# Modulation sums queued one chunk later, the gate summed in its own tile, and 24 modulation steps per sub-layer

## The chip, the cores and the metric

The kernel runs on one core of one Trainium2 chip. The metric is the device time of one launch in microseconds (us); the time before is the median of three runs.

## The reference, cut to what matters

Two layers of three sub-layers each: a half-step SwiGLU feed-forward, a token mixer (layer 0: sparse attention beside a gated delta rule, called "hybrid"; layer 1: multi-head latent attention), and another feed-forward. Every sub-layer is wrapped by a conditioning on one vector `c`:

```
cs  = silu(c)                                        # (1024,)
mod = cs @ mod_w[layer] + mod_b[layer]               # 9 x 1024: per sub-layer shift, scale, gate
x   = layer_norm(alpha * x + (1 + gate) * f(x * (1 + scale) + shift), ln_g, ln_b)
```

`x` is 256 x 1024, `mod_w[layer]` 1024 x 9216, a feed-forward has 2816 hidden columns; all is float32. The change concerns only how `cs @ mod_w + mod_b` (the modulation) is computed and when.

## The kernel before, in words

The six sub-layers si = 0 ... 5 run one after the other: feed-forward, hybrid, feed-forward, feed-forward, latent attention, feed-forward. A feed-forward (`ffn`) goes through 11 chunks of two tiles of 128 hidden columns. A chunk's gate and up products (matmuls into four banks of tag "gu", L263 to L265) are followed by silu on ScalarE (L548, `sg`), the product on VectorE (L551), a split of `h` in two parts, and, behind the next chunk's gate and up products, the down products (`acc<-hd,h`). Weights are split in two parts on ScalarE (L258) and VectorE or GpSimd (L259).

The modulation is a generator, `mod_gen`, that the sub-layers drive. For each sub-layer and each of scale (i = 1), shift (0) and gate (2), in this order, it makes eight steps: load 128 rows of `mod_w` (a 128 x 1024 tile, 512 KB, tag "wd" with three buffers, shared with the tiles of `ffn_w_down`), multiply by a column of `cs` and add into an accumulator (VectorE, L218 for the first step, L225 for the others). The accumulator (tag "macc", one buffer) then holds 128 partial rows; `mod_sums` adds them over the partitions at once. For scale and shift that is `mod_cols`: eight transposes on TensorE (L138) into two "gu" banks, and two reductions on VectorE (L139). For the gate it is `mod_gate`: two products with a matrix of ones (L180) into two "gu" banks, and on VectorE (L182) the sum is added to a tile G, which a DMA (L212) has filled with the gate's bias; G has two buffers. The epilogue of the sub-layer reads G (L381).

`pace` decides how many steps are traced beside which piece of a sub-layer. Its aim for the end of each sub-layer is a running count of steps, `goals`; inside a sub-layer the share grows with the tiles (feed-forward), with 14 "beats" (hybrid) or with the 16 heads (latent attention, eight of them for the whole share). When the share passes 1, `need` runs the generator until this sub-layer's gate and the next one's scale and shift are done.

The order on each engine is not the order of the program's text. A planner takes the instructions by the order in which they were traced, and issues an instruction on its engine as soon as, by the planner's own times, its inputs and a buffer are there; what was traced later fills the pauses of what was traced earlier, and may run far ahead of its place. Buffers of one tag are given out in the order of tracing. `behind(m)` lets what is traced in it be issued only behind the instruction `m` of the same engine. On the chip every engine then works through its queue in order: an instruction that waits holds up all behind it. `last_mm` is the last matmul that `mm3` has traced.

## Time and profile before

| what | value |
|---|---|
| median of three runs | 1216.07 us (1212.24 to 1216.48) |
| span of the profiled execution | 1212.3 us |
| VectorE busy | 905.5 us, 75% of the span |
| GpSimd busy | 255.4 us, 21% |
| moved by DMA | 259.76 MB, mean 214 GB/s |

The span runs from the first to the last instruction of one profiled execution. The page shows no time outside it; the median of the runs is 3.8 us above the span, and the fastest run lies 0.06 us below it. So the profiled execution's own time is taken as its span, and a difference worked out from its rows is applied to the median. In the rows, PE is TensorE, PEld its weight loads, DVE is VectorE, ACT is ScalarE, POOL is GpSimd, SP the queue that issues the DMAs. A line such as L225 is a line of the kernel.

### The profile page before, as it was taken

How to read it: one execution, taken by the hardware profiler on the slowest of the kernel's cores; microseconds unless marked ns; L12 is line 12 of the kernel's file. 1: busy time of each engine (PE TensorE's matmuls, PEld its weight loads, DVE VectorE, ACT ScalarE, POOL GpSimd, SP SyncE). 2: the span in 40 equal slices, each digit the busy share in tenths (PEclk: the TensorE clock that was granted, in tenths of full speed). 3: DMA queues.
4: the chain of work that ended last, by engine and by line, in shares of the span. 5: the costliest groups of instructions: out<-in, count | busy, mean ns of one | idle time of the engine just before them, and what ended most of it. 6: DMA issues, size and time to landing. Idle time of an engine off the chain costs nothing.

```text
span 1212.3 us, 19687 instructions
## 1 busy us (share of the span) xinstructions
PE 1135.4 (94%) x7783; PEld 1035.5 (85%) x7783; DVE 905.5 (75%) x1376; ACT 547.6 (45%) x959; POOL 255.4 (21%) x186
## 2 busy tenths in 40 slices
PE   4998999999899998999999899899989998999997
PEld 3897999788787887989999889799978878899995
DVE  6699777698985677878885888778788438866545
ACT  0644444456433445533543543334456556544430
POOL 0631000224731452320000322000221234300001
PEclk9999999999999999999999999999999998999999
DMA  9779999454310586788997488889725135876620
GB/s 352 249 260 345 303 319 303 145 165 123 98 36 5 188 274 212 243 291 297 325 307 238 139 283 284 269 297 302 266 79 168 66 105 180 295 250 189 215 72 35
DMA packets 155334, 259.76 MB, mean 214 GB/s; under 512 B 8813, under 2 KB 117354, under 8 KB 155242
## 3 DMA queue, kind: packets, MB, share of 16 engines
q1 hardware_dynamic: 155050, 258.45, 63.9%
q8 instruction: 61, 1.00, 0.3%
q14 instruction: 31, 0.25, 0.1%
q10 hardware_dynamic: 192, 0.05, 0.0%
HBM read 257.43 MB, written 1.05 MB: 213 GB/s over the span
## 4 chain that ended last, share of the span: by engine, by line
PE 51%; DVE 22%; DMA 13%; ACT 5%; issue 5%; POOL 3%; SPq 0%; POOLq 0%; DVEq 0%; ACTq 0%
PE gu L265 8%; PE gu L264 8%; PE gu L263 7%; DMA wd<-ffn_w_down 7%; PE acc L265 6%; PE acc L263 6%; PE acc L264 6%; DVE macc L225 3%; DMA wd<-mod_w 3%; DMA w<-ffn_w_up 2%; DVE g L259 2%; POOL hd L259 2%; PE gu L732 2%; DVE u L259 2%; ACT hd L258 1%
## 5 line engine op out<-in xcount | busy, mean ns | idle before, releaser
L225 DVE SCALAR_TENSOR_TENSOR macc<-wd,csT,macc 128x1024 f32<-128x1024 f32 x112 | 169.0, 1509 | 27.1 <-DMA wd<-mod_w 26.5
L263 PE MATMUL gu<-uT,g 128*128 128x256 f32 x640 | 181.1, 283 | 1.4 <-ACT sg L548 1.4
L265 PE MATMUL gu<-uT,g 128*128 128x256 f32 x640 | 181.2, 283 | 1.2 <-DVE g L259 1.2
L265 PE MATMUL gu<-uT,u 128*128 128x256 f32 x640 | 181.2, 283 | 1.0 <-DVE u L259 1.0
L263 PE MATMUL gu<-uT,u 128*128 128x256 f32 x640 | 181.1, 283 | 0.0
L264 PE MATMUL gu<-uT,u 128*128 128x256 f32 x640 | 181.1, 283 | 0.0
L264 PE MATMUL gu<-uT,g 128*128 128x256 f32 x640 | 181.1, 283 | 0.0
L258 ACT CAST hd<-wd 128x1024 fp32r<-128x1024 f32 x88 | 92.2, 1049 | 136.8 <-DMA wd<-ffn_w_down 118.9
L263 PE MATMUL acc<-hd,h 128*128 128x512 f32 x352 | 141.3, 401 | 1.5 <-ACT h L258 1.5
L265 PE MATMUL acc<-hd,h 128*128 128x512 f32 x352 | 137.6, 391 | 1.1 <-DVE h L259 1.1
L264 PE MATMUL acc<-hd,h 128*128 128x512 f32 x352 | 137.7, 391 | 0.0
L259 DVE TENSOR_TENSOR g<-w,g 128x1024 fp32r<-128x1024 f32 x86 | 118.9, 1386 | 22.8 <-ACT g L258 22.3
L263 PEld LDWEIGHTS gu<-uT,g 128*128 128x128 f32 x640 | 122.7, 192 | 3.2 <-ACT sg L548 1.8
L265 PEld LDWEIGHTS gu<-uT,g 128*128 128x128 f32 x640 | 122.7, 192 | 1.6 <-DVE g L259 1.6
L264 PEld LDWEIGHTS gu<-uT,g 128*128 128x128 f32 x640 | 122.7, 192 | 1.4
L265 PEld LDWEIGHTS gu<-uT,u 128*128 128x128 f32 x640 | 122.9, 192 | 1.2 <-DVE u L259 1.2
L263 PEld LDWEIGHTS gu<-uT,u 128*128 128x128 f32 x640 | 122.9, 192 | 0.0
L264 PEld LDWEIGHTS gu<-uT,u 128*128 128x128 f32 x640 | 122.9, 192 | 0.0
L259 DVE TENSOR_TENSOR u<-w,u 128x1024 fp32r<-128x1024 f32 x81 | 104.1, 1290 | 24.5 <-ACT u L258 24.3
L258 ACT CAST u<-w 128x1024 fp32r<-128x1024 f32 (+1 forms) x89 | 91.6, 1039 | 62.7 <-DMA w<-ffn_w_up 51.9
L259 POOL TENSOR_TENSOR hd<-wd,hd 128x1024 fp32r<-128x1024 f32 x32 | 86.6, 2712 | 141.6 <-ACT hd L258 141.6
L259 POOL TENSOR_TENSOR hl<-w,hl 128x1024 fp32r<-128x1024 f32 x28 | 72.5, 2602 | 202.2 <-ACT hl L258 201.7
(392 smaller groups left out, 2495.2 us busy)
## 6 DMA issues: line engine op xcount, KB each, us to landing
wd<-mod_w SPq DMA_DIRECT2D x130, 512.0 KB, 4.8
wd<-ffn_w_down SPq DMA_DIRECT2D x88, 512.0 KB, 4.6
w<-ffn_w_gate SPq DMA_DIRECT2D x43, 1024.0 KB, 8.3
w<-ffn_w_up SPq DMA_DIRECT2D x43, 1024.0 KB, 6.9
w<-hyb_w_in SPq DMA_DIRECT2D x16, 1024.0 KB, 6.1
w<-mod_w SPq DMA_DIRECT2D x7, 1024.0 KB, 7.5
w<-hyb_w_out SPq DMA_DIRECT2D x4, 1024.0 KB, 4.9
w<-mla_w_out SPq DMA_DIRECT2D x4, 1024.0 KB, 5.4
```

The costliest lines, as they stand in the source:

```text
L225: step = nc.vector.scalar_tensor_tensor(acc, w, c, acc, ALU.mult, ALU.add)
L258: i = self.nc.scalar.copy(hi, src)
L259: return i, (eng or self.nc.vector).tensor_tensor(out=lo, in0=src, in1=hi.bitcast(F32), op=ALU.subtract)
L263: nc.tensor.matmul(out, lh, rh, start=first, stop=False)
L264: nc.tensor.matmul(out, lh, rl, start=False, stop=False)
L265: self.last_mm = nc.tensor.matmul(out, ll, rh, start=False, stop=last)
L732: nc.tensor.matmul(pt[:, b * S : (b + 1) * S], q[:, b * P : (b + 1) * P], k, start=True, stop=True)
```

## The change: what it does

- `mod_sums` no longer follows its last step directly. When the eighth step is traced, the generator notes the last matmul traced so far (`held`) and stops; `pace` does not go on until `mm3` has traced another one. Then the sums are traced `behind` the newest matmul, on whichever engine they share with it (TensorE). `need` does not look at `held`.
- The gate is summed in its own tile: the accumulator is a tile of tag "G" (now one buffer), filled with the bias by DMA and multiplied by 1/128 on ScalarE, so that the sum over partitions holds the bias once. All eight steps are multiply-adds (L225). `mod_gate` copies the bank to that tile with 1 added, on ScalarE; the VectorE additions are gone.
- Scale and shift use "macc" with two buffers, for the first sub-layer too.
- `goals` 44, 64, 98, 132, 136, 144 become 40, 64, 88, 112, 136, 144: after the first, 24 steps in each sub-layer but the last, which has 8. In latent attention the share is spread over 14 heads rather than 8.
- Comments are removed, in many places; these hunks are left out here.

```diff
     def pace(self, part):
-        """runs the modulation up to its share of what this sub-layer takes of it"""
+
         goal = self.base + math.ceil((self.goal - self.base) * min(part, 1.0))
-        while self.count < goal:
+        while self.count < goal and (self.held is None or self.held is not self.last_mm):
+            self.held = None
             self.count += next(self.bg)
...
-    def mod_gate(self, si, acc, G):
-        """G holds the bias"""
+    def mod_gate(self, si, acc):
+
         nc = self.nc
         for h in range(2):
             pt = self.bank("gu")
             nc.tensor.matmul(pt, self.one, acc[:, h * 512 : (h + 1) * 512], start=True, stop=True)
-            g = G[:, h * 512 : (h + 1) * 512]
-            nc.vector.scalar_tensor_tensor(g, pt, 1.0, g, ALU.add, ALU.add)
-        self.G[si] = G
+            nc.scalar.activation(acc[:, h * 512 : (h + 1) * 512], pt, AF.Copy, bias=1.0)
+        self.G[si] = acc
...
-                acc = self.tl(self.wp, [P, D], "G", bufs=2) if si == 0 and i < 2 else self.tl(self.wp, [P, D], "macc")
                 if i == 2:
-                    G = self.tl(self.wp, [P, D], "G", bufs=2)
-                    nc.sync.dma_start(G, t["mod_b"][l, off : off + D].partition_broadcast(P))
+
+                    acc = self.tl(self.wp, [P, D], "G")
+                    nc.sync.dma_start(acc, t["mod_b"][l, off : off + D].partition_broadcast(P))
+                    nc.scalar.mul(acc, acc, 1.0 / P)
+                else:
+                    acc = self.tl(self.wp, [P, D], "macc", bufs=2)
...
-            if k == 0:
+            if k == 0 and i < 2:
                 nc.vector.tensor_scalar_mul(acc, w, c)
...
-            self.mod_sums(si, i, acc, G, step)
+            if self.last_mm is not None:
+                self.held = self.last_mm
+                yield 0
+                with self.behind(self.last_mm):
+                    self.mod_sums(si, i, acc, step)
+            else:
+                self.mod_sums(si, i, acc, step)
             self.mdone.add((si, i))
...
-            vs = self.tl(self.wp, [P, 2, 2, W], "macc")
+            vs = self.tl(self.wp, [P, 2, 2, W], "macc", bufs=2)
...
-        self.marks, self.last_mm = [None], None
+        self.marks, self.last_mm, self.held = [None], None, None
         self.left = None
-        goals = (44, 64, 98, 132, 136, 144)
+        goals = (40, 64, 88, 112, 136, 144)
...
-                T.pace((4 * g + i + 1) / 8)
+                T.pace((4 * g + i + 1) / 14)
```

## Rows read from the trace of the kernel before

**Rows 1.** The page, part 1: engine, busy us, share of the span, instructions.
```profile
PE 1135.4 (94%) x7783; PEld 1035.5 (85%) x7783; DVE 905.5 (75%) x1376; ACT 547.6 (45%) x959; POOL 255.4 (21%) x186
```
**Rows 2.** Busy time by stretch: stretch, length, engines, granted clock, DMA share, GB/s.
```profile
36.00:234.00 198.00, 191.59 (x1330) 177.87 (x1330) 157.71 (x208) 89.26 (x122) 37.12 (x50) 0.99 0.82 275
...
234.00:300.00 66.00, 59.16 (x398) 54.64 (x397) 57.78 (x138) 39.71 (x85) 19.88 (x10) 0.92 0.52 157
300.00:394.00 94.00, 86.55 (x643) 73.73 (x642) 72.67 (x152) 36.62 (x96) 40.13 (x28) 0.98 0.16 48
394.00:468.00 74.00, 72.77 (x464) 60.64 (x463) 52.65 (x78) 38.09 (x78) 34.13 (x15) 1.00 0.68 234
...
478.00:670.00 192.00, 188.83 (x1325) 176.53 (x1326) 150.03 (x177) 86.65 (x128) 25.15 (x12) 0.99 0.80 272
...
680.00:882.00 202.00, 194.59 (x1357) 181.54 (x1358) 162.11 (x190) 87.13 (x131) 29.42 (x14) 0.99 0.80 269
...
1010.00:1196.00 186.00, 184.68 (x1304) 173.85 (x1304) 115.34 (x139) 83.89 (x123) 22.71 (x10) 0.99 0.55 181
```
**Rows 3.** TensorE's timeline at four sums: start, us, line, tiles, [idle before <-releaser].
```profile
94.51 0.28 PE L265 MATMUL gu<-uT,u 128*128 128x256 f32 x1
98.99 3.65 PE L180 MATMUL gu<-macc,one 128*128 128x512 f32 x4 [4.19 <-DVE macc L225]
...
523.54 1.95 PE L180 MATMUL gu<-macc,one 128*128 128x512 f32 x4 [0.86 <-DVE macc L225]
...
559.90 0.63 PE L138 MATMUL gu<-ident,macc 128*128 128x128 f32 x4 [0.44 <-DVE macc L225]
561.27 0.66 PE L138 MATMUL gu<-ident,macc 128*128 128x128 f32 x4 [0.75 <-DVE sg L551]
...
761.49 0.66 PE L138 MATMUL gu<-ident,macc 128*128 128x128 f32 x4 [0.90 <-ACT sg L548]
765.16 1.11 PE L138 MATMUL gu<-ident,macc 128*128 128x128 f32 x4 [3.01 <-DVE sg L551]
```
**Rows 4.** Busy time by stretch, the two stretches of half clock (columns as Rows 2).
```profile
98.99:102.42 3.43, 3.43 (x5) 1.46 (x5) 2.20 (x5) 2.68 (x4) 0.00 (x0) 0.50 1.09 367
764.60:768.00 3.40, 2.84 (x9) 2.46 (x10) 3.40 (x7) 1.75 (x4) 0.00 (x0) 0.50 0.95 283
```
**Rows 5.** ScalarE's timeline before the sum at 761 us.
```profile
760.11 1.05 ACT L258 CAST u<-w 128x1024 fp32r<-128x1024 f32 x1 [7.21 <-DMA w<-ffn_w_up]
761.06 0.38 ACT L548 ACTIVATE sg<-gu 128x256 f32<-128x256 f32 x1
```
**Rows 6.** Tile macc: count, ns min/median/max, first and last start us, shapes.
```profile
L225 DVE SCALAR_TENSOR_TENSOR macc<-wd,csT,macc x112: 1271/1281/3431, 62.0 to 1133.4; 128x1024 f32<-128x1024 f32 x112
...
L218 DVE TENSOR_SCALAR macc<-wd,csT x16: 736/746/2241, 61.2 to 1019.0; 128x1024 f32<-128x1024 f32 x16
```
**Rows 7.** Tile G: its VectorE addition, and its DMA's landing.
```profile
L182 DVE SCALAR_TENSOR_TENSOR G<-gu,G x12: 675/684/692, 102.6 to 1189.9; 128x512 f32<-128x512 f32 x12
...
DMA to landing us min/median/max: 3.7/4.7/8.9
```
**Rows 8.** ScalarE groups: count, busy us, mean ns, idle before and its releasers.
```profile
L258 ACT CAST h<-sg 128x256 fp32r<-128x256 f32 x82 | 32.9, 405 | 146.3 <-DVE sg L551 146.3
...
L745 ACT COPY PT<-gu 128x512 f32<-128x512 f32 x12 | 7.0, 586 | 9.3 <-PE gu L743 9.3
...
L790 ACT ACTIVATE x<-x 128x1024 f32<-128x1024 f32 x2 | 2.0, 1052 | 0.0
```
**Rows 9.** VectorE's timeline: last step before, and first step after, the gated delta rule.
```profile
216.74 1.28 DVE L225 SCALAR_TENSOR_TENSOR macc<-wd,csT,macc 128x1024 f32<-128x1024 f32 x1
...
405.63 1.99 DVE L218 TENSOR_SCALAR macc<-wd,csT 128x1024 f32<-128x1024 f32 x1
```
**Rows 10.** TensorE's timeline: the gate sum of the hybrid.
```profile
403.11 1.88 PE L180 MATMUL gu<-macc,one 128*128 128x512 f32 x4
```
**Rows 11.** VectorE's timeline: the epilogue's last reading of G before the hybrid.
```profile
236.27 0.75 DVE L381 SCALAR_TENSOR_TENSOR tmp<-acc,G 128x256 f32<-128x256 f32 x2
```
**Rows 12.** GpSimd's timeline in the gated delta rule.
```profile
293.21 12.64 POOL L259 TENSOR_TENSOR hl<-w,hl 128x1024 fp32r<-128x1024 f32 x5 [10.24 <-ACT hl L258]
```
**Rows 13.** Busy time by stretch of latent attention (columns as Rows 2).
```profile
920.00:990.00 70.00, 68.79 (x479) 61.38 (x477) 34.80 (x107) 40.47 (x101) 14.34 (x6) 1.00 0.32 107
904.00:920.00 16.00, 14.00 (x105) 12.95 (x104) 15.63 (x40) 10.17 (x22) 6.07 (x11) 1.00 0.36 108
```

More of the change, by code (lines that the diff above doesn't have):

```diff
@@ L189, in mod_gen @@
         todo = [(si, i, k) for si in range(len(self.subs)) for i in (1, 0, 2) for k in range(KD)]
-        ws, loaded, G, step = {}, 0, None, None
+        ws, loaded, step = {}, 0, None
         def load(si, i, k):
@@ L234, in mod_gen, with mod_sums @@
                 self.load_x()
-    def mod_sums(self, si, i, acc, G, step):
+    def mod_sums(self, si, i, acc, step):
         if i == 2:
-            self.mod_gate(si, acc, G)
+            self.mod_gate(si, acc)
         elif i == 1:
```

## The prediction

> **What bounds the kernel now.** I read first the page's engine shares, then the busy times by stage, then TensorE's timeline wherever a modulation sum stands in it. TensorE is busy 1135.4 of 1212.3 us; ScalarE has 45% [rows 1]. So a change on VectorE or ScalarE pays only where TensorE stood still for it. The stages show where that can be. In the last feed-forward (8 modulation steps) TensorE is busy 184.68 of 186 us, 1.3 us idle. The first has 6.4 us idle (198 less 191.59), the third sub-layer 3.2 (192 less 188.83), the fourth 7.4 (202 less 194.59) [rows 2]. These three carry most of the steps, so I looked there at each sum.
>
> Four sums made TensorE wait, in two ways [rows 3]. The reader is to look at the bracket behind a row.
> - For the last step itself (releaser `macc`): 4.19 us at 98.99, 0.86 at 523.54, 0.44 at 559.90, together 5.49.
> - For a "gu" bank (releaser `sg`): the two banks of a sum are those that the chunk's own silu and product must first empty. 0.75 us at 561.27, 0.90 and 3.01 at 761.49 and 765.16, together 4.66.
>
> The two longest were followed by stretches with the granted clock at 0.50, that is 1.2 instead of 2.4 GHz, of 3.43 and 3.40 us [rows 4]; each costs about half its length, 1.7 us. So the sums' places hold 5.49 + 4.66 + 3.4 = 13.6 us. This is the most that the change can gain in the feed-forwards.
>
> **The change part by part.**
>
> *Sums a chunk later.* In a feed-forward `last_mm` changes once a chunk, so a held sum stands behind the next chunk's gate and up products. A chunk lasts about 17 us (an estimate: the 186 us of the last feed-forward over 11 chunks [rows 2]). The step that was late by 4.19 us will have ended long before. All the `macc` waits go: 5.49 us, and the first half-clock stretch with them, 1.7. What is late next at that place is the bank: the sum still stands directly behind a chunk's products and still needs the first two banks, so the `sg` waits are not touched by the placing. They hang on how far ScalarE and VectorE lag. At 761 ScalarE had stood 7.21 us for a tile of `ffn_w_up`, with the silu queued behind it [rows 5]: a late DMA, in a stage whose DMA share is 0.80 against 0.55 in the last feed-forward [rows 2]. Ten of its modulation tiles go (5.2 MB of the 54 MB or so that 269 GB/s over 202 us make), so this gets rarer, not impossible. Bounds: none of 4.66 + 1.7 = 6.4 us, or all. I take half, 3.2. Gain of the placing: 5.5 + 1.7 + 3.2 = 10.4 us.
>
> *The gate in its own tile.* Per gate VectorE loses two additions of 0.684 us [rows 7] and its first step grows from 0.746 to 1.281 [rows 6]: 0.83 us less, 5 us over six gates. TensorE does not wait for these in a feed-forward, so nothing is booked. ScalarE gains per gate a multiplication of 128 x 1024, 1.05 us by the nearest row, and two copies out of a bank at 0.59 [rows 8]: 2.2 us, 13 over six. It stood 146.3 us for `sg` alone [rows 8]; that idle time hides it. Without that cover a gate would cost its 2.2 us.
>
> The multiplication is a new wait on ScalarE, for the bias DMA, which lands 4.7 us after issue in the median and 8.9 at most [rows 7]. Queued behind it stand casts and silu, and TensorE waits for these. The DMA is traced ahead of the gate's weight tiles and is normally early. Bounds 0 and 8.9 us once; I take 0. On SP the same DMA now waits for the only G buffer, until the epilogue before has read it; behind it on SP stand the following weights. The epilogue of the first feed-forward reads G last at 236.27 [rows 11], and the hybrid's modulation is traced after that, so the wait is short.
>
> *24 steps per sub-layer.* The feed-forwards lose 4, 10 and 10 steps, the hybrid gains 4 and latent attention 20. Where VectorE is not what TensorE waits for, the steps saved are worth nothing.
>
> In the hybrid the place changes more than the number. Before, VectorE ran no step between 216.74 and 405.63 [rows 9], because the single `macc` buffer was held until the gate sum got its banks at 403.11 [rows 10]; after it 16 steps ran beside attention. Now the gate's eight steps can start only behind 236.27 (one G), and scale and shift have two more buffers. The planner fills VectorE's pauses with whatever has its inputs; the four gate steps traced in the hybrid already ran before 217 us. So part of the 24 steps can move into the gated delta rule (234 to 394), where VectorE is busy 57.78 of 66 and 72.67 of 94 us and TensorE idles 6.8 and 7.5 us [rows 2]. No row shows a step there. The nearest row is attention, 394 to 468: with 16 steps among its work TensorE idled 74 less 72.77 = 1.23 us in all, at most 0.08 per step. By this 24 steps cost 1.9 us. From above, a step that delays TensorE by its full 1.281 us costs that much each; with 16 of them in the delta rule, 20.5 us. From below, everything that TensorE idled in attention, 1.2 us, could be won. I take 1.9, the nearest row.
>
> In latent attention VectorE is full early (15.63 of 16 us, 904 to 920) and half idle later (34.80 of 70, 920 to 990) [rows 13]. 24 steps are 31 us, 1.7 steps per head, and 35 us are free from 920 on. The planner has them behind the heads, so few fall into the full stretch. By the same 0.08 the cost is 1.9 us. Bounds: 0, and for six steps that all delay TensorE in the full stretch, 7.7. The sums there (gate, scale, shift) are TensorE work that moved from the feed-forward before, so it cancels.
>
> *Sum*: 10.4 gained, 1.9 + 1.9 lost: 6.6 us less. On the profiled span 1212.3 gives 1205.7; on the median, 1216.07 less 6.6 = 1209.5.
>
> **A rule that speaks against it.** A step's median is 1.281 us, its longest 3.431 [rows 6], and GpSimd works 12.64 us without a pause from 293.21 in the delta rule [rows 12]. By the Trainium skill (SBUF — State Buffer, "Who interferes with whom") a VectorE instruction with two SBUF inputs and a GpSimd instruction that reads SBUF share a port, and the later one waits for the whole of the other. The long steps agree with it; it would put 3.4 instead of 1.3 us on a step that lands in such a stretch. Whether steps land there no run has shown; this is part of the second rival.
>
> **The rivals.**
>
> *The bank waits stay, and the result drowns.* For it: both kinds of wait end at the same place, and the `sg` waits depend on silu, which the change does not hurry; after a hold `pace` catches up three or four steps in a row (4 x 1.281 = 5.1 us on VectorE), which can make `sg` late elsewhere. Against it: less DMA in these stages. Then the gain is 5.5 + 1.7 = 7.2, less 3.8: 3.4 us, 1212.7.
>
> *Steps in the gated delta rule (slower).* Mechanism: the freed buffers let steps run from 240 to 394, and the short chain between VectorE and TensorE there is lengthened at each. Price: 1.281 us a step. 16 steps cost 20.5; with 1.9 in latent attention and 10.4 gained that is 12 us more, 1228. It turns the sign from (10.4 - 1.9) / 1.281, about 7 such steps, on. For it: TensorE's 14 us of idle time show that it waits there, and VectorE has few pauses. Against it: these steps go only where the planner sees a pause, and a delay can be swallowed by projections that TensorE has queued between.
>
> *All waits at sums go and attention pays nothing*: 13.6 us less, 1202.5. For it: attention's TensorE hardly idles. Against it: some bank wait always remains.
>
> **How the numbers follow.** The runs of the kernel spread over 0.35%; about 0.5% (6.1 us) can be told from no change. Chances: forecast 0.35 (1209.5, its own range 1204 to 1213), all waits gone 0.13, bank waits stay 0.30, delta rule slower 0.22. The forecast stands just beyond 0.5%, so a part of it (0.06) counts as no change, and a part of the slower rival (0.03) with few steps too. Faster 0.42, within 0.5% 0.39, slower 0.19. The range goes from 1200 (the 13.6 us and a little DMA relief) to 1225 (close to the slower rival), leaving out about 0.1 on either side.
>
> **What the profile after would show.** Right: no bracket "DVE macc" before L138 or L180 on TensorE in a feed-forward; no half clock at the first gate sum; idle time of TensorE in the fourth sub-layer well under 7 us; steps within latent attention with TensorE's idle time there up by no more than 2 us. Wrong, first rival: brackets with `sg` before the sums, as long as now. Wrong, second rival: L225 rows between 240 and 394 us, and the stretches 234 to 300 and 300 to 394 longer by over 5 us. The forecast falls altogether if a new wait of several us on ScalarE for the bias DMA shows up.

## The result: 2.6% slower, where 0.5% faster was forecast

The changed kernel takes 1247.37 us in the median of four runs (1243.07 to 1254.21), the kernel before on the same chip 1216.28 (1212.24 to 1219.44): a ratio of 1.026, interval 1.023 to 1.0291. That is 31 us more where 6.6 less were forecast, and 22 us beyond the range's end.

The profiled execution has a span of 1252.4 us against 1212.3. It is the slowest of the changed kernel's four runs (mean granted clock 0.965, where the fastest, 1243.07 us, has 0.976), so the stages below add up to 40 us of difference where the medians show 31. I cut both into stages at TensorE's first transposes of each sub-layer's input rows (`gu<-ident,x`), and added up TensorE's idle time and the stretches of granted clock 0.50 (1.2 GHz) in each. Lengths in us, before to after; the other columns are worked out in the same way:

| stage | length | difference | TensorE idle | at clock 0.50 |
|---|---|---|---|---|
| first feed-forward | 214.8 to 217.5 | +2.7 | 8.2 to 9.3 | 3.4 to 6.8 |
| hybrid | 239.6 to 260.8 | **+21.2** | 16.2 to 27.2 | 13.7 to 37.5 |
| second feed-forward | 201.2 to 203.3 | +2.2 | 4.0 to 6.8 | 3.4 to 6.8 |
| third feed-forward | 207.2 to 206.0 | -1.2 | 10.5 to 8.8 | 3.4 to 6.8 |
| latent attention | 123.1 to 136.4 | **+13.3** | 9.9 to 13.4 | 0.5 to 17.1 |
| last feed-forward | 204.8 to 206.8 | +2.0 | 10.4 to 12.0 | 10.3 to 11.9 |

I count half of a stretch at half clock as lost, an estimate from the two granted clocks, 0.50 and 1.00. In the hybrid 11.0 us more of idle time and half of 23.8 us more of half clock give 22.9, near the 21.2; in latent attention 3.5 and half of 16.6 give 11.8 of 13.3. So of this execution's 40 us the two attentions lost about 34, and by this count some 20 of them by the clock.

The page's part 1 of after, to compare with [rows 1]: VectorE works no more than before, TensorE 22 us more in as many matmuls.

```profile
PE 1157.3 (92%) x7783; PEld 1054.1 (84%) x7783; DVE 905.9 (72%) x1364; ACT 562.4 (45%) x977; POOL 262.6 (21%) x186
```

The busy times by stretch (stretch, length, PE, PEld, DVE, ACT, POOL, granted clock, DMA share, GB/s). The hybrid is cut at the last matmul of the scan (the loop over four chunks of rows that ends the gated delta rule). First the kernel before:

```profile
236.40:392.60 156.20, 143.72 (x1025) 126.97 (x1026) 128.05 (x285) 74.41 (x175) 60.01 (x37) 0.96 0.31 94
392.60:476.00 83.40, 79.76 (x503) 66.55 (x502) 60.16 (x90) 39.75 (x83) 37.25 (x17) 1.00 0.68 231
```

And after, with the latent attention and a feed-forward behind it that answer to [rows 2, 13]:

```profile
239.00:409.10 170.10, 148.39 (x1039) 131.27 (x1040) 147.27 (x299) 76.25 (x177) 60.68 (x37) 0.94 0.44 135
409.10:499.80 90.70, 85.20 (x489) 70.86 (x489) 47.75 (x81) 40.93 (x84) 35.97 (x17) 0.91 0.51 174
...
704.00:906.00 202.00, 195.19 (x1351) 181.79 (x1350) 149.65 (x172) 92.61 (x140) 30.83 (x14) 0.98 0.70 234
...
922.00:1026.00 104.00, 95.65 (x635) 86.41 (x634) 87.41 (x189) 52.91 (x130) 29.09 (x22) 0.95 0.64 212
```

The reader is to see two things. The delta rule has 19 us more of VectorE work (147.27 against 128.05: 14 modulation steps) and lasts 14 us longer. But the rest of the hybrid has 12 us *less* VectorE work and still lasts 7 us longer, with the granted clock at 0.91 instead of 1.00. "So many more steps" can't be the whole cause.

**What the forecast had looked at** did happen. TensorE's timeline at the first gate sum, and what ended TensorE's idle time before all the transposes of the sums [rows 3]:

```profile
131.23 2.28 PE L181 MATMUL gu<-G,one 128*128 128x512 f32 x4
```

```profile
L139 PE MATMUL gu<-ident,macc x80: 270/273/329, 190.4 to 1020.8; 128*128 128x128 f32 x80
its engine sat idle before it (us, times) until:
  DVE sg L560: 0.2, 1
```

No `macc` bracket is left, the `sg` waits are 0.2 us instead of 4.66, and the clock at the first gate sum stays at 1.00. Other waits of the same size stand elsewhere in the feed-forwards: transposes for the rotary angles waiting for a bank, and a silu behind a late tile of `ffn_w_up`. Half clock of 3.4 us follows the first (from 138.02), and 6.8 us begins within the second (from 530.56).

```profile
137.66 0.33 PE L680 MATMUL gu<-ident,cs 128*128 128x128 f32 x1 [4.03 <-DVE sg L560]
...
532.54 0.58 PE L272 MATMUL gu<-uT,g 128*128 128x256 f32 x1 [4.47 <-ACT sg L557]
```

**In the delta rule** VectorE's timeline shows the steps that [rows 9] had none of: six of the gate from 247.35 to 301.68 and eight of scale from 308.31 to 385.34. ScalarE's multiplication of the bias stands at the very head of the hybrid, among the casts of its input.

```profile
247.35 1.28 DVE L228 SCALAR_TENSOR_TENSOR G<-wd,csT,G 128x1024 f32<-128x1024 f32 x1 [0.68 <-ACT G L213]
...
301.68 3.00 DVE L228 SCALAR_TENSOR_TENSOR G<-wd,csT,G 128x1024 f32<-128x1024 f32 x1
308.31 2.61 DVE L221 TENSOR_SCALAR macc<-wd,csT 128x1024 f32<-128x1024 f32 x1 [0.29 <-DMA wd<-mod_w]
...
385.34 1.28 DVE L228 SCALAR_TENSOR_TENSOR macc<-wd,csT,macc 128x1024 f32<-128x1024 f32 x1
```

```profile
246.26 1.06 ACT L213 ACTIVATE G<-G 128x1024 f32<-128x1024 f32 x1
```

**At the end of the delta rule** the last normalisation (`decT`, four instructions on VectorE) takes 7.50 us, beside three GpSimd splits (of weights, L268) of 7.15 us together; attention's first logits (`lg`) are behind it on VectorE, and TensorE waits 3.14 us for them. The granted clock is then 0.50 for 17 us, in which TensorE is never idle. VectorE, GpSimd, TensorE and the stretch:

```profile
415.01 7.50 DVE L1315 SCALAR_TENSOR_TENSOR decT<-decT,oss,ngz 128x128 f32<-128x128 f32 x4 [8.58 <-POOL oss L120]
422.55 0.42 DVE L745 CUSTOM_DVE_ANT_0 lg<-gu,sc 128x256 f32<-128x256 f32 x1
```

```profile
414.95 7.15 POOL L268 TENSOR_TENSOR hl<-w,hl 128x1024 fp32r<-128x1024 f32 x3
```

```profile
423.67 0.44 PE L752 MATMUL gu<-ident,lg 128*128 128x128 f32 x2 [3.14 <-ACT lg L750]
```

```profile
424.70:441.80 17.10, 17.10 (x64) 13.51 (x63) 4.37 (x11) 4.29 (x11) 0.00 (x0) 0.50 0.28 104
```

Before, the same normalisation ran from 396.29 for 5.47 us while TensorE still had projections queued until the gate sum at 403.11 [rows 10], and no `lg` was due:

```profile
396.29 5.47 DVE L1306 SCALAR_TENSOR_TENSOR decT<-decT,oss,ngz 128x128 f32<-128x128 f32 x4 [6.56 <-POOL oss L119]
```

**In latent attention** two steps stand on VectorE beside the division of four heads (L762, L764), and the transposes behind it wait 1.89 us; 3.4 us at 0.50 begin at 967.46, as this wait ends, and 3.4 more follow a wait of 1.61 us at 990. VectorE and TensorE:

```profile
964.78 1.28 DVE L228 SCALAR_TENSOR_TENSOR G<-wd,csT,G 128x1024 f32<-128x1024 f32 x1
965.98 0.20 DVE L762 RECIPROCAL sums<-sums 128x8 f32<-128x8 f32 x1
966.10 0.70 DVE L221 TENSOR_SCALAR macc<-wd,csT 128x1024 f32<-128x1024 f32 x1
966.83 0.69 DVE L764 TENSOR_TENSOR PT<-acc,sums 128x512 f32<-128x512 f32 x1
```

```profile
967.58 1.11 PE L768 MATMUL gu<-ident,PT 128*128 128x128 f32 x4 [1.89 <-DVE PT L764]
```

Before, no step ran in latent attention, and of these transposes the longest wait there was 0.31 us. The other half clock in this stage does not stand behind the division: 6.8 us at its head (from 909.44), ahead of its first step at 918.5, and 3.4 us at 933.33.

### The profile page after: what moved, and what is told of

It reads as the page before. It is cut to its first block, busy times and chain, and to the rows that moved or that the text cites. A ratio compares the mean times of both kernels' runs of the same rounds, so it can differ in the third digit from the quotient of the medians.

```text
span 1252.4 us, 19669 instructions
## 1 busy us (share of the span) xinstructions
PE 1157.3 (92%) x7783; PEld 1054.1 (84%) x7783; DVE 905.9 (72%) x1364; ACT 562.4 (45%) x977; POOL 262.6 (21%) x186
## 4 chain that ended last, share of the span: by engine, by line
PE 60%; DVE 20%; DMA 9%; ACT 4%; issue 4%; POOL 3%; SPq 0%; POOLq 0%; DVEq 0%; ACTq 0%
PE gu L272 10%; PE gu L274 10%; PE gu L273 10%; PE acc L274 7%; PE acc L272 7%; PE acc L273 7%; DVE G L228 2%; PE gu L741 2%; DMA wd<-ffn_w_down 2%; DMA wd<-mod_w 2%; DMA w<-ffn_w_gate 2%; DVE g L268 2%; DVE u L268 1%; DMA w<-ffn_w_up 1%; DMA w<-mod_w 1%
## 5 line engine op out<-in xcount | busy, mean ns | idle before, releaser
L274 PE MATMUL acc<-hd,h 128*128 128x512 f32 x352 | 140.0, 398 | 3.1 <-DVE h L268 3.1
L272 PE MATMUL acc<-hd,h 128*128 128x512 f32 x352 | 141.7, 402 | 0.0
L273 PE MATMUL acc<-hd,h 128*128 128x512 f32 x352 | 140.0, 398 | 0.0
L268 DVE TENSOR_TENSOR g<-w,g 128x1024 fp32r<-128x1024 f32 x86 | 118.5, 1383 | 25.8 <-ACT g L267 25.8
L228 DVE SCALAR_TENSOR_TENSOR macc<-wd,csT,macc 128x1024 f32<-128x1024 f32 x72 | 97.1, 1349 | 43.7 <-DMA wd<-mod_w 43.3
L268 DVE TENSOR_TENSOR u<-w,u 128x1024 fp32r<-128x1024 f32 x81 | 104.0, 1288 | 28.1 <-ACT u L267 28.0
L268 POOL TENSOR_TENSOR hl<-w,hl 128x1024 fp32r<-128x1024 f32 x28 | 72.6, 2600 | 230.1 <-ACT hl L267 230.1
L268 POOL TENSOR_TENSOR hd<-wd,hd 128x1024 fp32r<-128x1024 f32 x32 | 88.2, 2764 | 121.2 <-ACT hd L267 121.2
```

Source lines behind the costliest of these rows:

```text
L228: step = nc.vector.scalar_tensor_tensor(acc, w, c, acc, ALU.mult, ALU.add)
L268: return i, (eng or self.nc.vector).tensor_tensor(out=lo, in0=src, in1=hi.bitcast(F32), op=ALU.subtract)
L272: nc.tensor.matmul(out, lh, rh, start=first, stop=False)
L273: nc.tensor.matmul(out, lh, rl, start=False, stop=False)
L274: self.last_mm = nc.tensor.matmul(out, ll, rh, start=False, stop=last)
```

## The experiments

Ratios are against runs of the kernel before on the same chip, whose medians were 1214.13 to 1217.03 us. The profiled execution gives each stage's length; differences from before in us (FF: feed-forward). Each stage difference comes from one execution, while the ratios come from four to six runs of a kernel (two for sums at once, short steps and no loads). Where the two disagree, the ratio is the firmer number:

| kernel | ratio [95%] | FF 1 | hybrid | FF 2 | FF 3 | latent | FF 4 |
|---|---|---|---|---|---|---|---|
| changed kernel | 1.0260 [1.0230, 1.0291] | +2.7 | +21.2 | +2.2 | -1.2 | +13.3 | +2.0 |
| held sums alone | 1.0100 [1.0074, 1.0125] | +2.7 | +9.7 | +2.6 | -2.3 | +2.0 | -0.1 |
| held, feed-forwards only | 1.0040 [1.0023, 1.0058] | +4.6 | 0.0 | +3.2 | +0.1 | +2.3 | +0.1 |
| gate's own tile alone | 1.0055 [1.0030, 1.0080] | +1.0 | -2.1 | +4.7 | +0.9 | +0.7 | +0.8 |
| held and own tile | 1.0154 [1.0116, 1.0193] | +6.9 | +0.5 | +5.6 | +0.4 | +1.8 | +1.0 |
| new goals alone | 1.0142 [1.0120, 1.0164] | +8.3 | +2.9 | -1.0 | +0.9 | +11.1 | -1.8 |
| own tile, new goals | 1.0118 [1.0090, 1.0146] | +2.0 | +0.9 | +4.7 | +3.3 | +7.2 | +0.7 |
| changed, sums at once | 1.0269 [1.0239, 1.0300] | -1.2 | +18.4 | +3.7 | -3.8 | +12.5 | +5.6 |
| changed, old buffers | 1.0414 [1.0394, 1.0435] | +15.2 | +19.4 | +3.9 | +4.6 | +6.3 | +0.2 |
| changed, steps fenced | 1.0250 [1.0226, 1.0274] | +0.2 | +22.0 | +2.6 | -2.4 | +11.4 | +0.1 |
| changed, short steps | 1.0164 [1.0137, 1.0192] | +2.1 | +12.4 | -1.6 | -3.0 | +7.5 | +1.0 |
| changed, no loads | 1.0308 [1.0287, 1.0329] | +4.6 | +15.9 | +0.6 | +1.6 | +12.8 | +3.2 |
| changed, no multiplication | 1.0243 [1.0225, 1.0262] | +2.4 | +20.1 | +0.5 | -2.2 | +13.5 | +1.5 |
| nothing left of the steps | 1.0142 [1.0125, 1.0160] | +6.3 | +10.2 | +1.4 | -3.1 | +4.7 | +0.4 |
| fenced, no multiplication | 1.0207 [1.0161, 1.0253] | +4.9 | +9.0 | +0.3 | -4.2 | +13.3 | +1.1 |
| nothing left, fenced | 1.0062 [1.0039, 1.0086] | +4.2 | -2.3 | +1.8 | -2.7 | +5.1 | +1.7 |

### One part alone

**Held sums**, in the kernel before:

```diff
-        while self.count < goal:
+        while self.count < goal and (self.held is None or self.held is not self.last_mm):
+            self.held = None
...
-            self.mod_sums(si, i, acc, G, step)
+            if self.last_mm is not None:
+                self.held = self.last_mm
+                yield 0
+                with self.behind(self.last_mm):
+                    self.mod_sums(si, i, acc, G, step)
```

> The kernel before with nothing but the held sums. Both theories: the waits for the last step (5.5 us) and the half clock behind the first gate sum (1.7 us) go, bank waits stay or go: 1203 to 1210. If the sums' waits only move to other places: 1216.

1228.45 us, outside both expectations. Of the feed-forwards only the third is clearly shorter, by 2.3, and the hybrid costs 9.7 more: with one `macc` buffer a held sum holds up the steps of the next sum, and TensorE waits 7.80 us for their end.

```profile
444.40 1.97 PE L139 MATMUL gu<-ident,macc 128*128 128x128 f32 x8 [7.80 <-DVE macc L226]
```

To see what holding is worth where it was meant to pay, it was switched off in hybrid and latent attention (`if self.last_mm is not None and self.subs[self.si][1] != 1:`).

> The kernel before with held sums in the feed-forwards alone; in hybrid and latent attention at once. If the holding costs by delaying the hybrid's gate sum, and with it the only macc buffer: hybrid back to 240 us, and the feed-forwards keep what they gained: 1208 to 1214. If the holding costs in the feed-forwards too: 1216 to 1222.

1219.87 us: no gain. The stall of 4.19 us at the first gate sum [rows 3] is gone, and the first feed-forward is 4.6 us longer all the same, with 2.52 us of waiting at 223.92 and 3.43 at its end that were shorter before.

**The gate's own tile**, in the kernel before, with its two buffers for G and one for `macc`:

```diff
-                    G = self.tl(self.wp, [P, D], "G", bufs=2)
-                    nc.sync.dma_start(G, t["mod_b"][l, off : off + D].partition_broadcast(P))
+                    acc = self.tl(self.wp, [P, D], "G", bufs=2)
+                    nc.sync.dma_start(acc, t["mod_b"][l, off : off + D].partition_broadcast(P))
+                    nc.scalar.mul(acc, acc, 1.0 / P)
...
-            g = G[:, h * 512 : (h + 1) * 512]
-            nc.vector.scalar_tensor_tensor(g, pt, 1.0, g, ALU.add, ALU.add)
+            nc.scalar.activation(acc[:, h * 512 : (h + 1) * 512], pt, AF.Copy, bias=1.0)
```

> The kernel before with the gate summed in its own tile alone (multiplied bias, copies on ScalarE; two buffers for G, one for macc, sums at once, the old goals). The prediction booked nothing for it: 1211 to 1219, every stage within 2 us. Rival (the gate's own tile brings its share of the loss, since its steps need not wait for macc and move): a feed-forward 4 us or more longer, total 1221 to 1235.

1221.48 us, 0.3 to 0.8% slower, so the rival holds by a little: the second feed-forward is 4.7 us longer. There ScalarE stands 5.02 us for a late tile of `ffn_w_up`, with the cast of `h` queued behind it, and TensorE 5.70 for that cast; before, its longest wait in this part of the stage was 1.10. ScalarE and TensorE:

```profile
506.98 1.99 ACT L260 CAST u<-w 128x1024 fp32r<-128x1024 f32 x2 [5.02 <-DMA w<-ffn_w_up]
508.88 0.36 ACT L260 CAST h<-acc 128x256 fp32r<-128x256 f32 x1
```

```profile
509.30 0.80 PE L265 MATMUL acc<-hd,h 128*128 128x512 f32 x1 [5.70 <-ACT h L260]
```

The new multiplication and copies are not in these waits. Why this tile comes late here is not shown. **Held sums and own tile together** (both diffs, old goals):

> The changed kernel (held sums, gate summed in its own tile) with the goals, the latent pace and the buffers of before (two G, one macc). Theory A (steps that run ahead into the gated delta rule cost the time, and the 20 steps more in latent attention the rest): latent attention is as before; macc is no longer held by the gate, so the scale steps of the next sub-layer can still run ahead into 240 to 394 us, some 8 of them: about 1216, that is 10 us gained at the sums and up to 10 lost there. Theory B (the number of steps per sub-layer alone decides, wherever they stand): hybrid and latent attention as before, the sums' gain shows: about 1206.

1234.53 us, above what either theory expected: the loss lies in the first two feed-forwards, and the attentions are nearly untouched. **The new goals alone** (`goals = (40, 64, 88, 112, 136, 144)`, and 14 for 8 in latent attention):

> The kernel before with nothing but the new goals and the latent pace over 14 heads. Theory A: with one macc buffer, held until the gate sum, no scale or shift step can run ahead, so the delta rule stays as before and only latent attention pays, 13 us: about 1229. Theory B: hybrid (+24 us) and latent attention (+13 us) pay as in the changed kernel, and the sums gain nothing: 1247 or more.

1233.35 us, 11.1 of it in latent attention, 2.9 in the hybrid, and 8.3 in the first feed-forward, which has four steps *less*. In latent attention it is the wait seen in the changed kernel: three things stand in front of the division on VectorE, two of them steps, and TensorE waits 3.97 us. VectorE and TensorE:

```profile
968.08 1.28 DVE L225 SCALAR_TENSOR_TENSOR macc<-wd,csT,macc 128x1024 f32<-128x1024 f32 x1
969.28 0.20 DVE L753 RECIPROCAL sums<-sums 128x8 f32<-128x8 f32 x1
969.40 1.28 DVE L225 SCALAR_TENSOR_TENSOR macc<-wd,csT,macc 128x1024 f32<-128x1024 f32 x1
970.72 0.69 DVE L755 TENSOR_TENSOR PT<-acc,sums 128x512 f32<-128x512 f32 x1
```

```profile
971.46 0.90 PE L759 MATMUL gu<-ident,PT 128*128 128x128 f32 x3 [3.97 <-DVE PT L755]
```

So each part alone is slower. None of them alone costs the hybrid 21 us; the held sums cost it 9.7.

### What in the hybrid costs 21 us

**The steps fenced out of the delta rule**, in the changed kernel:

```diff
-                nc.vector.tensor_tensor(out=vn[r], in0=u[b][r], in1=v3(pv)[r], op=ALU.subtract)
+                self.fence = nc.vector.tensor_tensor(out=vn[r], in0=u[b][r], in1=v3(pv)[r], op=ALU.subtract)
...
-        self.T.pace(self.beats / 14)
+        with self.T.behind(self.fence):
+            self.T.pace(self.beats / 14)
```

> The changed kernel with one addition: in the hybrid, modulation steps are queued on VectorE behind the last VectorE instruction of the gated delta rule. Theory A: the stretch from 238 us to the end of the delta rule goes back to its length of before (16 us less) and the half clock in attention with it (up to 8 us): about 1223 to 1231. Theory B: the hybrid's 24 steps now all stand beside attention, the time stays at 1247 or grows.

1247.21 us: no step stands in the delta rule, its scan still ends 7.7 us late, and the hybrid costs 22.0. Taken as it stands, this speaks against the second rival. **Short steps** (the hybrid's and latent attention's multiply-adds take 8 of 1024 columns; the rest of their products is left out):

```diff
-                step = nc.vector.scalar_tensor_tensor(acc, w, c, acc, ALU.mult, ALU.add)
+                n8 = 8 if self.subs[self.si][1] == 1 else D
+                step = nc.vector.scalar_tensor_tensor(acc[:, 0:n8], w[:, 0:n8], c, acc[:, 0:n8], ALU.mult, ALU.add)
```

> The changed kernel, but a multiply-add traced in the hybrid or in latent attention adds 8 of its 1024 columns (what is left out: the other columns, so that scale, shift and gate of three sub-layers miss products). All loads, sums, goals and buffers stay. Theory A' (VectorE time of the steps in front of each mixer's own chain is the cost): hybrid 240 to 247 us and latent attention 123 to 126, against 260.8 and 136.4 in the changed kernel; whole kernel about 1220. Theory C (the cost is the loads, the sums or the order): both lengths stay within 3 us of the changed kernel's.

1233.79 us, between the two expectations: the edit is worth 8.8 us of the hybrid's 21.2 and 5.8 of latent attention's 13.3. The order of instructions changed with it (see below), so this is not VectorE's time alone. **No loads** (seven of eight loads of these steps left out, `acc` multiplied in place of the tile; VectorE's work stays):

```diff
-                load(*todo[loaded])
+                if todo[loaded] not in skip:
+                    load(*todo[loaded])
...
-            w, c = ws.pop((si, i, k)), self.cs[:, k : k + 1]
+            w, c = acc if (si, i, k) in skip else ws.pop((si, i, k)), self.cs[:, k : k + 1]
```

> The changed kernel, but of the steps that belong to the second sub-layer's gate, the next scale and shift, and the same three of latent attention, seven of eight load no tile of mod_w and read their accumulator instead (what is left out: these products; VectorE works as long as before). Theory A': hybrid and latent attention stay long, 255 or more and 133 or more. Theory C, if it is the loads: both go back, about 242 and 124.

1251.21 us, no shorter than the changed kernel, and the hybrid still +15.9: the loads aren't the main cause. **Sums at once** (the diff of the held sums undone in the changed kernel):

> The changed kernel with the sums traced at once as before, the rest of the change kept (gate in its own tile, buffers, goals, latent pace). Theory A': hybrid and latent attention stay long, above 255 and 133, since the steps stand where they stood. If the holding is what costs there (it bunches three or four steps after each sum): the hybrid comes down by 10 us or so, as the held sums alone added 9.7 to it. The feed-forwards get their waits at the sums back, up to 13 us in the first, third and fourth sub-layer.

1246.54 us, the hybrid still +18.4: nor is the holding. **Old buffers** (`"G", bufs=2` for one, and `"macc"` with one for two):

> The changed kernel with two buffers for G and one for macc, as before; held sums, the gate in its own tile and 24 steps per sub-layer stay. Theory (the second macc buffer is what lets scale and shift run their steps without waiting for a sum, and the single G what brings the gate's steps and multiplication to the head of the hybrid): the delta rule is back near its old length, its scan ends within 3 us of before (156.2 us from the hybrid's start; changed kernel 170.1), and the hybrid costs at most 10 us more instead of 21; latent attention keeps its 11 to 13 us, since the goals are the same. Total about 1230 to 1238. Rival (the number of steps and the held sums do it, with any buffers): the scan ends 8 us late or more, the hybrid stays at +18 to +22, total 1242 to 1250.

1264.91 us, a miss for my theory: the hybrid stays at +19.4. And the first feed-forward has 15.2 more: with a second G the hybrid's gate steps run among the first epilogue's instructions (steps of 4.62 and 2.81 us on VectorE between those of L390 and L393), and TensorE waits 11.5 us for the epilogue's output:

```profile
251.18 1.12 PE L291 MATMUL gu<-ident,x 128*128 128x128 f32 x4 [11.50 <-ACT x L414]
```

**No multiplication of the bias** (`nc.scalar.mul(acc, acc, 1.0 / P)` left out; the gate's bias then counts 128 times):

> The changed kernel without the multiplication of the bias by 1/128 on ScalarE (the gate then holds 128 times its bias). Theory (this multiplication, a wait for a DMA and 1.05 us at 8 us into the hybrid among the casts of its input, sets the delta rule back): the first products of the delta rule's keys come 4 us earlier than in the changed kernel (90.4 us from the hybrid's start, before 82.5), the hybrid costs 13 to 17 us instead of 21, total about 1240 to 1243. Rival (it is hidden; the steps and the order they force are what costs): hybrid still +19 to +23, total 1245 to 1251.

1245.17 us: by itself it is hidden. **Nothing left of the steps** (short steps, no loads and no multiplication put together):

> The changed kernel with the steps of the hybrid and of latent attention cut to 8 of 1024 columns, seven of eight of their loads left out and the bias not multiplied by 1/128: of the modulation only its 48 short instructions, its sums and the gate's copies are left in these two sub-layers, traced where they are in the changed kernel. Theory (VectorE's steps, loads and the multiplication together are the cost, and overlap so that one taken away shows little): hybrid within 4 us of before, latent attention within 3 us, total about 1218 to 1224. Rival (the order in which the planner puts everything else, with sums at other places, and the half clock behind them cost by themselves): hybrid +8 to +13, latent +5 to +8, total 1230 to 1236.

1232.20 us. With hardly any of the steps' work left, 10.2 us in the hybrid and 4.7 in latent attention stay.

### The order of the delta rule's own instructions

I then compared, engine by engine, the order of the delta rule's instructions and of those that run beside it with the kernel before, and set it beside the moment at which the scan ends (us from the hybrid's start; before 156.2). Of VectorE's 228 instructions here, 110 are the rule's and its gates', 48 the q, k and v projections', 52 the sparse attention's selection of rows (`index`), and 18 others. "Moved" are those of the 228 that fall out when the two sequences are matched block by block, longest first. The counts below are taken from the traces; the recorded expectations count in the built programs, and have 42 for the fenced kernel and 3 for the two that show 0 here:

| kernels | moved on VectorE | scan ends at |
|---|---|---|
| held; held in feed-forwards; own tile; both; new goals | 0 | 155.0 to 156.9 |
| own tile, new goals; fenced, no multiplication; nothing left, fenced | 0 | 155.8; 156.2; 155.8 |
| nothing left; fenced; short steps | 40; 40; 45 | 161.7; 163.9; 163.8 |
| no loads; sums at once; changed kernel | 61; 61; 68 | 167.4; 167.3; 170.1 |
| no multiplication; old buffers | 71; 82 | 171.5; 169.2 |

So the kernels that keep the order end the scan at 155.0 to 156.9, and those that do not at 161.7 to 171.5. Of the 68 that moved in the changed kernel, 37 are the rule's and its gates', 15 the selection's and 12 the projections'. Matched by themselves, only 9 of the 110 of rule and gates moved there, and 3 in the kernels with 40 and 45: what changes is mostly how the rule, the projections and the selection are interleaved. "Fenced" and "nothing left" have the same order of these instructions on all four engines, though no step runs in the rule in the one, and six of 0.22 us each in the other; their scans end 2.2 us apart. "No loads" and "sums at once" share another order, and end 0.1 us apart.

The planner puts an instruction where its own times leave a pause. Three more kernels were built to part order from work; their rows stand in the table too. The first had the fence and lacked the multiplication (the gate's bias counts 128 times), which leaves the order of before:

> The changed kernel with the hybrid's steps queued behind the delta rule's last VectorE instruction, and without the multiplication of the bias by 1/128 (the gate then holds 128 times its bias). In the built program the delta rule's own 637 instructions then stand in the order of the kernel before on every engine but for three at its end, where the changed kernel has 68 of VectorE's 228 and 23 of ScalarE's 119 at other places, and the kernel with the steps fenced alone 42 and 15. Theory (it is this order, tipped by any modulation work among the hybrid's first instructions, that sets the delta rule back): the scan ends within 2 us of before (156.2 us from the hybrid's start) where the fence alone had 163.9; the hybrid costs +10 to +15, all of it in attention, total 1233 to 1240. Rival (the hybrid's steps are paid wherever they stand, as the fence alone seemed to show): hybrid +19 to +23, total 1243 to 1249.

1238.68 us. The scan ends at 156.2, exactly as before. Against the fence alone the hybrid is 13.0 us shorter (261.6 to 248.6), where the multiplication by itself had been worth 1.1. The medians of the two kernels differ by less, 8.5 us, and the intervals of their ratios overlap. What is left lies in attention: VectorE takes the fenced steps among the normalisation and in front of the first `lg`, and TensorE waits 6.14 us. VectorE and TensorE:

```profile
400.19 2.50 DVE L1315 SCALAR_TENSOR_TENSOR decT<-decT,oss,ngz 128x128 f32<-128x128 f32 x1 [1.89 <-POOL oss L120]
402.62 1.27 DVE L227 SCALAR_TENSOR_TENSOR G<-wd,csT,G 128x1024 f32<-128x1024 f32 x1
403.81 7.30 DVE L1315 SCALAR_TENSOR_TENSOR decT<-decT,oss,ngz 128x128 f32<-128x128 f32 x3
411.04 3.91 DVE L227 SCALAR_TENSOR_TENSOR G<-wd,csT,G 128x1024 f32<-128x1024 f32 x3
414.99 0.42 DVE L744 CUSTOM_DVE_ANT_0 lg<-gu,sc 128x256 f32<-128x256 f32 x1
```

```profile
416.11 0.69 PE L751 MATMUL gu<-ident,lg 128*128 128x128 f32 x2 [6.14 <-ACT lg L749]
```

The second is "nothing left" with the fence: the same modulation work as there; what differs is the place of the short steps, and with it the order.

> The kernel with nothing of the steps left in the hybrid and latent attention but 8 of 1024 columns (no multiplication of the bias, seven of eight loads left out), with the hybrid's short steps queued behind the delta rule. The modulation's work is the same as in that kernel, and only the order differs: the delta rule's instructions stand as in the kernel before (three moved, there 40 of VectorE's 228). Theory (order): the scan ends within 2 us of before, the hybrid +2 to +6 instead of +10.2, total 1222 to 1228. Rival (the 10.2 us come from the sums and the gate's copies, which both kernels have): hybrid +9 to +12, total 1229 to 1234.

1221.77 us, and the hybrid below the +2 to +6 expected. The stretches of "nothing left" (first two from the hybrid's start to the scan's end, third to the hybrid's end):

```profile
241.80:327.00 85.20, 72.74 (x507) 67.90 (x508) 72.75 (x166) 52.99 (x134) 37.41 (x22) 0.93 0.52 153
327.00:404.00 77.00, 73.12 (x527) 61.12 (x526) 56.41 (x125) 22.13 (x42) 23.73 (x15) 0.96 0.11 32
404.00:492.00 88.00, 82.67 (x501) 69.85 (x500) 38.06 (x82) 41.06 (x85) 34.15 (x17) 0.94 0.40 134
```

and of the same with the fence:

```profile
239.60:321.00 81.40, 71.78 (x504) 66.89 (x505) 69.81 (x160) 52.94 (x134) 34.54 (x22) 0.94 0.51 153
321.00:396.00 75.00, 71.25 (x529) 59.12 (x528) 61.66 (x133) 21.72 (x42) 25.49 (x16) 1.00 0.10 30
396.00:477.00 81.00, 78.62 (x502) 66.38 (x501) 38.61 (x89) 40.93 (x85) 34.25 (x17) 1.00 0.49 162
```

The hybrid is 12.6 us shorter with equal work, 2.3 less than before: in the first two stretches 5.8, in attention 7.0, where the clock is 1.00 against 0.94. The medians differ by 10.4 us, and no run of the one is as long as any of the other (1220.69 to 1223.13 against 1229.83 to 1234.19). The edit moves six short steps, 1.3 us on VectorE in all, out of the head of the delta rule (and eight more out of the first feed-forward) to its end; that is too little work for 10 us, and "fenced", with no step there but the same order, ends the scan late as well. So the order that the steps force costs the hybrid 10 to 13 us. Which of the moved instructions cost it was not taken apart. Four kernels now form a square:

| hybrid, difference from before | steps with their work | hardly any work |
|---|---|---|
| order with 40 moved | +22.0 (fenced) | +10.2 (nothing left) |
| order of before | +9.0 (fenced, no multiplication) | -2.3 (nothing left, fenced) |

Of the four only "fenced" keeps the multiplication of the bias, worth 1.1 us by itself. The work is worth 11.8 or 11.3 us, the order 13.0 or 12.6, each nearly the same whatever the other is. The third kernel has the gate's own tile and the new goals, sums at once, two buffers for G and one for `macc`; its order is that of before:

> The changed kernel with sums at once and with two buffers for G and one for macc: the gate in its own tile and 24 steps per sub-layer. The delta rule's instructions stand in the order of before. Theory (order): the scan ends within 2 us of before, the hybrid at +2 to +6, as with the goals alone (+2.9); latent attention +8 to +13 (24 steps); total 1230 to 1238. Rival (the gate's own tile with 24 steps is what costs the hybrid its 18 to 21 us, in whatever order): hybrid +15 or more, total 1245 to 1255.

1229.41 us, the hybrid at +0.9 with 24 steps per sub-layer. There, as before the change, no step runs in the delta rule (none from 225 to 405 us): six of the gate's eight run in the first feed-forward, so that 18 of the 24 fall in the hybrid (16 before the change, 24 in the changed kernel). Latent attention pays 7.2.

Put beside its neighbours, this kernel also says which parts bring the steps in. With the gate's own tile and the new goals, the held sums alone are enough ("old buffers", scan 169.2), and so are the new buffers alone ("sums at once", 167.3); with neither the order stays (155.8), and with held sums, own tile and the old goals it stays too ("both", 155.6). No kernel beat the one before.

## Why the prediction was wrong

**What bounds the kernel:** TensorE's waits in the feed-forwards were read rightly row by row; the hybrid was read by its idle time alone.

**Sums a chunk later: 10.4 us booked, nothing earned.** The mechanism is as described: no `macc` bracket, hardly an `sg` wait, no half clock at the first sum. But the first three feed-forwards together are 3.7 us longer, and holding alone in the feed-forwards gives 0.2 to 0.6% more. The step that failed is that a wait taken away shortens its stage: others of the same size come up, for a bank (4.03 us) and for a late tile of `ffn_w_up` (4.47), and more half clock. Why just these come is not settled; over the kernels tried here a feed-forward's length differs from before by -4.2 to +15.2 us.

**The gate in its own tile: 0 booked, about 6 us measured alone** (0.3 to 0.8%). The named risk, ScalarE's multiplication, is not in the waits of that kernel, and without it the changed kernel stays within its interval. It is not harmless, though: with the steps fenced, taking it out brings the old order back.

**24 steps per sub-layer, with the buffers that let them run early: 3.8 us booked, 34 lost by hybrid and latent attention in the profiled execution.** This is the step by which the forecast falls. The price of 0.08 us per step was TensorE's idle time in attention divided by its 16 steps, and was applied to steps that stand elsewhere. It left out three things.
- *Order.* The forecast spoke of pauses that the planner fills. It did not see that a step traced near the delta rule also pushes the instructions of the rule and of what runs beside it into another order, which costs even when the step is shortened to almost nothing: 12.6 us of the hybrid between two kernels of equal work (10.4 by their medians), 13.0 between the two with full steps (8.5).
- *Steps in attention.* With the order restored, "fenced, no multiplication" pays 9.0 us for steps that stand before `lg`, and 11.3 more than the same without work. Work of 11 to 12 and order of 13, less the 2.3 of the kernel that has neither, give the fenced kernel's 22.0. The changed kernel has the same loss (21.2) with 68 moved in place of 40 and 14 of its steps in the delta rule; by how much each of the two counts there was not taken apart.
- *The clock.* Over half of the loss in each is granted clock 0.50. In the hybrid 17.1 of the 23.8 us more are the stretch read above, behind the wait of 3.14 us; in latent attention 6.8 of the 16.6 are the two behind the division. The rest stands elsewhere, 6.8 us of it at the head of latent attention before any step. The forecast had priced the clock at the feed-forwards' sums [rows 4] and not here.

In latent attention the bound of 7.7 was for steps in its early stretch. They came later, beside the division, where VectorE is half idle: the free time says nothing of who is due next. "Nothing left" shows 8.6 of its 13.3 us to be the steps' work and loads; the remaining 4.7 to 5.1 were not taken apart (sums and gate copies that moved here from the third feed-forward are a candidate; that stage is 2.7 to 3.1 shorter in the same kernels).

**The second rival** named the place and the sign: 14 steps run between 240 and 394 us, and the stretch is 13.9 longer; 1.281 us each would make 17.9. Its mechanism holds in part only, since the kernel that takes the steps out of the delta rule, with 40 instructions moved all the same, loses as much (fenced, +22.0). The "against" that I gave it, that steps go only where the planner sees a pause, was wrong: the planner's times are not the chip's. That no row showed a step there I read as "cheap by the nearest row"; it should have raised the question what kept the steps out. The forecast named the single `macc`, held until 403 [rows 10]. That is not enough: in "gate's own tile alone" and in "own tile, new goals" the gate does not use the one `macc`, and still no step runs in the delta rule; in the first a step wrote `macc` at 220.4 us, and its next followed at 405.9. What kept the steps out stays open.

**The rule on the shared port** (the Trainium skill, SBUF — State Buffer, "Who interferes with whom"): the step at 301.68, with two tiles as inputs, took 3.00 us instead of 1.28 beside a GpSimd split of 2.39 at 301.20, and three of the four `decT` instructions took 2.44 to 2.49 us beside splits, the last, with none beside it, 0.34. The trace agrees. The step at 308.31, with one tile and a column as inputs, is not of the kind that the rule as quoted speaks of, and took 2.61 instead of 0.75 beside a split of 2.40 at 307.96 all the same. For these two steps the loss on VectorE is 3.6 us.

## What to carry to other kernels

Before moving filler work into a stage that waits on a chain of short instructions, ask what has kept it out. Where a planner orders instructions, compare the order of the chain, and of what is interleaved with it, before and after; if it changed, price that first, by two runs with the filler's work removed, one in the old order and one in the new. And a stall removed from a stage that runs close to its loads is a gain only when the stage's length says so.

## What was unexpected of the hardware

A wait of 3.14 us on TensorE was followed by 17 us of granted clock 0.50, although TensorE then had no idle time at all (the row of 424.70 above); a wait of 1.89 in latent attention was followed by 3.4 us. In the fenced kernel without multiplication a wait of 6.14 us stands at the same place as the 3.14, with 6.8 us at 0.50 that begin within it, and its whole hybrid has 17.1 us at 0.50 against 37.5: in these traces the longer wait came with less half clock. And one VectorE instruction on 128 x 128 (`decT`) took 0.34 us where it began with no GpSimd split running, and 2.44 to 2.51 us beside a split of 2.4 us. Of the four in a row, two fell beside a split before the change (5.47 us in all), and three in the changed kernel (7.50).
